# Splitting the first down-projection rows ahead of the last convolutions, in four pairs of slots

## The chip, the cores and the metric

The kernel runs on one core of a Trainium2 chip. It has a matrix engine (TensorE, PE in the profile), a vector engine (VectorE, DVE), a scalar engine (ScalarE, ACT), a general one (GpSimd, POOL) and a queue engine that issues the transfers (SyncE, SP). Each works through its own instructions in order. The metric is the device time of one execution in microseconds, the median of several runs.

## The reference, cut to what matters

One layer of a trunk: two recurrent mixers, and behind them a feed-forward block with a convolution. Only that block matters here:

```python
def _conv_ffn(h, w_up, conv_w, w_down, rows, cols):
    u = _dwconv2d(h @ w_up, conv_w, rows, cols)
    a, b = jnp.split(u, 2, axis=-1)
    return (jax.nn.silu(a) * b) @ w_down
...
    xl = xl + g2 * _conv_ffn(_modulate(_rmsnorm(xl, norm2_w[l]), sh2, sc2), w_up[l], ffn_conv_w[l],
                             w_down[l], rows, GRID_W)
    return _rmsnorm(xl, final_norm_w)
```

There are 1024 tokens of width 1024, the inner width is 2816 (22 blocks of 128), and the convolution is 3 x 3 over a 16 x 64 grid, one filter per channel.

## The kernel before

All matrix products are made in three matmuls of rounded parts: a factor x is held as xh (a cast to the fp32r format, on ACT) and xl = x - xh (a subtraction, called a split here, on DVE or POOL), and the product is xh wh + xh wl + xl wh. The weights get wh on ACT and wl on POOL in the same way.

The block's first loop runs over j = 0 to 21. For each j, `up(j)` and `up(22 + j)` multiply the input (kept in the 16 tiles L0 to L15: part k of it has its high half in L(2k) and its low half in L(2k+1)) into PSUM tiles of 128 channels x 1024 tokens, 48 matmuls each. `conv2` then makes the convolution: one scaled copy on ACT (L1483) and eight multiply-adds on DVE (L1490), each reading the tile before it. The first of the two goes into G[j] and through a Silu (L1548), the second into a tile cb, and POOL multiplies them (L1552). In the last j the PSUM tiles are copied to SBUF first (src, L1531), so that the down-projection can have their banks.

The second loop, the down-projection, runs over two halves `dh` of the output columns, and in each over c = 0 to 21, the rows of w_down in blocks of 128. `down_ops(c, dh, kind)` loads the weights (one transfer for two c), casts and splits them, casts G[c] (L1522) and splits it (L1523); 24 matmuls follow (L1575). For kind 1 the two halves of G[c] lie in slots of the tag L, which the input of the up-projection held before: L0, L1 for even c and L2, L3 for odd ones. For c = 0 of the first half (kind 0) there is a pair of tiles of its own. Slots of a weight cast are four, of a weight transfer three.

Who works when: PE's order in the down-projection is the text's. All other engines, and PE in the up-projection, get their order from a planner that walks through the program with estimated durations before the kernel is built; its order on each engine is then fixed. On the chip an engine whose next instruction isn't ready waits, with all that stands behind it.

At the end of the first half, DVE takes the result out of PSUM (L1595) and adds it to the residual (L1600), ACT squares it (L1602) and POOL multiplies it by a weight (L1611).

Of the kernel before, what the change touches and what calls it, by code (L numbers as in the profile page):

```python
# [10 lines left out]
F32R = mybir.dt.float32r  # L11
I32 = mybir.dt.int32
AF = mybir.ActivationFunctionType
ALU = mybir.AluOpType
# [3 lines left out]
P = 128  # L18
D = 1024
KD = D // P  # L20
T = 1024
# [9 lines left out]
NF = DFF // P  # L31
# [37 lines left out]
WARM = 4  # L69
NL = 4  # L70
NGL = 9
MOVE = ((0, 1, 2, 3), (4, 5, 6, 7))


@with_exitstack
def kernel(ctx: ExitStack, tc: tile.TileContext, A: dict, out: bass.AP):
# [3 lines left out]
    V, S, G, PE, SY = nc.vector, nc.scalar, nc.gpsimd, nc.tensor, nc.sync  # L80

    def pool(name, bufs=1, space=None, side=None):
        kw = {}
        if space is not None:
            kw["space"] = space
        if side is not None:
            kw["side"] = side
        return tc.tile_pool(name=name, bufs=bufs, **kw)
# [7 lines left out]
    def raw(ap):  # L96
        return ap.bitcast(F32)
# [24 lines left out]
    gd = dp.tile([P, P], F32, name="gd")  # L122
# [27 lines left out]
    def pl_tile(name):  # L150
        return ps2.tile([P, T], F32, name=name, tag="pl")
# [245 lines left out]
    pls = [pl_tile("pv0"), pl_tile("pv1")]  # L397
# [27 lines left out]
    pls = [pl_tile("pv0"), pl_tile("pv1")]  # L425
# [93 lines left out]
    def bcast_cols(dst, cols_, tiles):  # L519
        for g in range(2):  # L520
            p_ = tiles[g]
            for j in range(4):
                k = 4 * g + j
                PE.matmul(p_[:, j * P:(j + 1) * P], cols_[:, k:k + 1].to_broadcast([P, P]), ident, start=True, stop=True)
            S.copy(dst[:, g * 512:(g + 1) * 512], p_)
# [109 lines left out]
    with ExitStack() as es:  # L635
# [204 lines left out]
        def ml_prep(h, qt):  # L840
            Wt = []
            Qs = []
            for d in range(2):
                g4 = ml4.tile([P, NLT, P], F32, name="g4", tag="w4")
                SY.dma_start(out=g4, in_=gdv[h, d * 16 + NCX:d * 16 + NCH, :].partition_broadcast(P))
                w4 = ml4.tile([P, NLT, P], F32, name="w4t", tag="w4")
                V.tensor_tensor(w4, g4, mmask[:, d, :].unsqueeze(1).to_broadcast([P, NLT, P]), op=ALU.max)
                for c in range(NLT):
                    S.activation(w4[:, c, :], w4[:, c, :], AF.Exp, scale=-1.0, bias=U[:, d, NCX + c, h:h + 1])
                G.tensor_tensor(g4, g4, M[:, d, NCX:NCH, h:h + 1].to_broadcast([P, NLT, P]), op=ALU.subtract)  # L850
                S.activation(g4, g4, AF.Exp, scale=-1.0)
                V.tensor_tensor(g4, g4, qt.rearrange("p (c t) -> p c t", c=NLT), op=ALU.mult)
                Wt.append(w4)
                Qs.append(g4)
            return Wt, Qs
# [110 lines left out]
        pre = ml_prep(0, cur["q"])  # L966
        run(rnd1)
        flips = None
        for h in range(H):
# [10 lines left out]
            last = h == H - 1  # L980
            hs_ = ml_scan(h, cur, fill, RL if last else (R0 if h == 0 else R1), pre)
            pre = None
# [360 lines left out]
    with ExitStack() as es:  # L1343
# [94 lines left out]
        for ct in (0, NF):  # L1438
            halves = wq.pop(0)
            pl = pl_tile("pu")  # L1440
# [12 lines left out]
    def big_tile(i, name):  # L1453
        return pl_tile(name) if i % 4 < 2 else psb.tile([P, T], F32, name=name, tag="plb")


    lo = ctx.enter_context(pool("lo", side="left"))
    low = [[lo.tile([P, T], F32R, name=f"low{i}", tag=f"L{i}") for i in range(q, 2 * KD, 2)] for q in range(2)]
    Gp = ctx.enter_context(pool("G", side="left"))
    Gt = [Gp.tile([P, T], F32, name=f"G{j}") for j in range(NGL)]  # L1460
    g2bc = Gp.tile([P, D], F32, name="g2bc")
    with ExitStack() as es:
        fp = es.enter_context(pool("ff", bufs=2, side="left"))
        f1 = es.enter_context(pool("ff1", bufs=1, side="left"))
        bt = big_tile(2, "bt")
        bcast_cols(g2bc, mod2[:, 3 * KD:4 * KD], (bt[:, 0:512], bt[:, 512:1024]))
        fcw = f1.tile([P, 2 * NF, 9], F32, name="fcw")
        SY.dma_start(out=fcw, in_=A["ffcw"].rearrange("p (a b) -> p a b", b=9))

        def up(ct):  # L1470
            j, b = ct % NF, ct // NF
            if j == 0:
                return early[b][0]
            halves = split_weights(A["wup"][ct])
            pl = big_tile(2 * j + b, "pu")
            for g in range(2):
                up_half(pl, halves, g)
            return pl

        def conv2(acc, src, wcol):  # L1480
            a3 = acc.rearrange("p (r c) -> p r c", c=GW)
            s3 = src.rearrange("p (r c) -> p r c", c=GW)
            S.activation(acc, src, AF.Copy, scale=wcol(4))  # L1483
            for dy in (0, -1, 1):
                for dx in (-1, 0, 1):
                    if dy == 0 and dx == 0:
                        continue
                    r0, r1 = max(0, -dy), GH - max(0, dy)
                    c0, c1 = max(0, -dx), GW - max(0, dx)
                    V.scalar_tensor_tensor(  # L1490
                        a3[:, r0:r1, c0:c1], s3[:, r0 + dy:r1 + dy, c0 + dx:c1 + dx],
                        wcol((dy + 1) * 3 + dx + 1), a3[:, r0:r1, c0:c1], op0=ALU.mult, op1=ALU.add)

        pst = {}

        def g_pool(j):
            return Gp if j < NGL else Gr

        def down_ops(c, dh, kind):
            if c % 2 == 0:  # L1500
                st = wp.tile([P, 2, 512], F32, name="wst", bufs=3)
                SY.dma_start(out=st, in_=A["wdown"][dh, c // 2].rearrange("p (a b) -> p a b", a=2))
                pst["s"] = st
                if kind == 2:
                    pst["w"] = [g_pool(c - NF + NL + i).tile([P, 2, 512], F32R, name="wd", tag=f"G{c - NF + NL + i}")
                                for i in range(2)]
            src = pst["s"][:, c % 2, :]
            if kind == 2:
                wh, wl = [w[:, c % 2, :] for w in pst["w"]]
                gh, gl = [g_pool(j).tile([P, T], F32R, name="gd", tag=f"G{j}")  # L1510
                          for j in range(NL + 2 * (c - NF + NL), NL + 2 * (c - NF + NL) + 2)]
            else:
                wh = wp.tile([P, 512], F32R, name="wh", bufs=4)
                wl = wp.tile([P, 512], F32R, name="wl", bufs=4)
                if kind:
                    gh, gl = [lo.tile([P, T], F32R, name="gd", tag=f"L{2 * (c % 2) + i}") for i in range(2)]
                else:
                    gh = Gr.tile([P, T], F32R, name="gh")
                    gl = Gr.tile([P, T], F32R, name="gl")
            S.copy(wh, src)  # L1520
            G.tensor_tensor(wl, src, raw(wh), op=ALU.subtract)  # L1521
            S.copy(gh, Gt[c])  # L1522
            (G if dh == 0 and c < 3 else V).tensor_tensor(gl, Gt[c], raw(gh), op=ALU.subtract)  # L1523
            return gh, gl, wh, wl

        def up_src(ct, last):
            pl = up(ct)
            if not last:
                return pl
            src = fp.tile([P, T], F32, name="src", tag="cb")  # L1530
            S.copy(src, pl)  # L1531
            return src

        for j in range(NF):
            if j < len(MOVE):
                for k in MOVE[j]:
                    SY.dma_start(out=raw(low[0][k]), in_=raw(h2h[k]))
                    SY.dma_start(out=raw(low[1][k]), in_=raw(h2l[k]))
            if j == len(MOVE) + 1:
                h2h[:], h2l[:] = low  # L1540
                h2_cm.__exit__(None, None, None)
                Gr = ctx.enter_context(pool("Gr", side="right"))
                Gt.extend(Gr.tile([P, T], F32, name=f"G{i}") for i in range(NGL, NF))
            if j == NF - 1:
                pre0 = down_ops(0, 0, 0)
            pl = up_src(j, j == NF - 1)
            conv2(Gt[j], pl, lambda i: fcw[:, j, i:i + 1])
            S.activation(Gt[j], Gt[j], AF.Silu)  # L1548
            pl = up_src(NF + j, j == NF - 1)
            cb = fp.tile([P, T], F32, name="cb", tag="cb")  # L1550
            conv2(cb, pl, lambda i: fcw[:, NF + j, i:i + 1])
            G.tensor_tensor(Gt[j], Gt[j], cb, op=ALU.mult)  # L1552


# [5 lines left out]
    ms_cm.__enter__()  # L1560
    ys = [lo.tile([P, D], F32, name=f"y{t}", tag=f"L{4 + t}") for t in range(NLT)]
    s0 = d1.tile([P, NLT, 2], F32, name="s0")
    pre = [pre0]
    for dh in range(2):
        ds_ = slice(dh * 512, (dh + 1) * 512)
        pp = [big_tile(i, "pd") for i in range(NLT // 2)]
# [2 lines left out]
        def part(c, last, dh=dh):  # L1569
            return down_ops(c, dh, 2 if last else 1)  # L1570
# [34 lines left out]
        if dh == 0:  # L1605
            order = (0, 4, 1, 5, 2, 6, 3, 7)
            tmps = [evac(t) for t in order]
            pre = [part(c, False, 1) for c in range(2)]
# [109 lines left out]
```

## Time and profile before

| | us |
|---|---|
| median of 3 runs | 1572.02 (1570.85 to 1574.15) |
| profiled execution, own time | 1571.65 |
| its span | 1569.8 |
| PE busy | 1498.0 (95%) |
| DVE busy | 1112.2 (71%) |
| ACT busy | 543.4 (35%) |
| POOL busy | 599.6 (38%) |
| up-projection matmuls end | 1305.66 |

The up-projection with its convolutions takes the third quarter of the span, the down-projection the last 264 us. Times in the views are microseconds from the start of the span. Idle time of an engine costs only where the engine that bounds the stretch stands still with it.

### The profile page before, as it was taken

What the parts mean: (1) busy time and instruction counts of PE and PEld (TensorE: products, weight loads), DVE (VectorE), ACT (ScalarE), POOL (GpSimd) and SP (SyncE); (2) the same over time, 40 slices, a digit from 0 to 9 for tenths busy, and PEclk for the clock granted to TensorE, in tenths of its full rate; (3) what the DMA queues carried; (4) which work ended last, traced back from release to release, by engine and by line L of the source; (5) the groups of instructions that cost most, each with busy time, mean ns of one, the idle gap of its engine ahead of it and who ended that gap; (6) DMA issues with size and microseconds to landing.
All of it is one profiled execution on the core that took longest, in us unless ns stands there. A gap on an engine that the chain in (4) does not pass through costs nothing.

```text
span 1569.8 us, 22515 instructions
## 1 busy us (share of the span) xinstructions
PE 1498.0 (95%) x8934; PEld 1216.9 (78%) x8934; DVE 1112.2 (71%) x1460; ACT 543.4 (35%) x949; POOL 599.6 (38%) x510
## 2 busy tenths in 40 slices
PE   7899999998999999999999999999999998998997
PEld 4667788887877777777867888888888886886886
DVE  5777667779486776766587988989889898226334
ACT  4443243444143243434454222222222223233332
POOL 0073244554244644433322433332333325335341
PEclk8999999999999999999999999999999999999999
DMA  9246430222031111125567111111111104111102
GB/s 377 84 145 199 145 98 28 80 68 55 33 119 55 56 42 44 39 82 173 176 213 287 41 54 41 54 50 45 54 41 54 52 30 160 58 50 41 51 30 108
DMA packets 47935, 141.78 MB, mean 90 GB/s; under 512 B 4947, under 2 KB 15059, under 8 KB 47830
## 3 DMA queue, kind: packets, MB, share of 16 engines
q1 hardware_dynamic: 47830, 140.35, 26.5%
q8 instruction: 70, 1.15, 0.3%
q14 instruction: 35, 0.29, 0.1%
HBM read 119.81 MB, written 12.13 MB: 84 GB/s over the span
## 4 chain that ended last, share of the span: by engine, by line
PE 70%; DVE 7%; POOL 3%; ACT 3%; issue 2%; DMA 1%; POOLq 0%; SPq 0%; ACTq 0%; DVEq 0%
PE pu L1429 30%; PE pd L1575 13%; PE po L1285 3%; PE pl_hg L509 3%; PE pl_zb L509 3%; PE pl_zf L509 3%; PE pl_mo L509 2%; PE pl_mq L509 2%; PE pc L509 1%; PE pl_hq L509 1%; PE ap L1088 1%; DVE G L1490 1%; POOL QQ L1125 1%; PE st L876 1%; PE pl_mk L509 1%
## 5 line engine op out<-in xcount | busy, mean ns | idle before, releaser
L1429 PE MATMUL pu<-low,wh 128*128 128x512 f32 x1216 | 374.2, 389 | 0.0
L133 ACT CAST wh<-wst 128x512 fp32r<-128x512 f32 x184 | 112.0, 620 | 527.9 <-issue 227.2
L135 POOL TENSOR_TENSOR wl<-wst,wh 128x512 fp32r<-128x512 f32 x114 | 150.8, 1325 | 356.0 <-ACT wh L133 343.0
L1429 PEld LDWEIGHTS pu<-low,wh 128*128 128x128 f32 x1216 | 228.2, 188 | 47.4
L1429 PE MATMUL pu<-low,wl 128*128 128x512 f32 x608 | 236.5, 389 | 0.0
L1490 DVE SCALAR_TENSOR_TENSOR G<-pu,fcw,G 128x945 f32<-128x945 f32 (+2 forms) x168 | 205.3, 1222 | 23.9 <-ACT G L1483 19.1
L1490 DVE SCALAR_TENSOR_TENSOR cb<-pu,fcw,cb 128x945 f32<-128x945 f32 (+2 forms) x168 | 205.3, 1222 | 23.6 <-ACT cb L1483 18.8
L1575 PE MATMUL pd<-wh,gd 128*128 128x512 f32 x624 | 195.8, 395 | 11.6 <-DVE gd L1523 6.7
L1523 DVE TENSOR_TENSOR gd<-G,gd 128x1024 fp32r<-128x1024 f32 x41 | 56.8, 1386 | 129.7 <-ACT gd L1522 129.5
L1575 PEld LDWEIGHTS pd<-wh,gd 128*128 128x128 f32 x624 | 118.8, 191 | 37.9 <-DVE gd L1523 7.8
L1125 POOL TENSOR_TENSOR QQ<-QQ,FF 128x256 f32<-128x256 f32 x112 | 108.8, 993 | 80.7 <-PE ap L1088 38.0
L1429 PEld LDWEIGHTS pu<-low,wl 128*128 128x128 f32 x608 | 114.1, 188 | 23.7
L1575 PE MATMUL pd<-wl,gd 128*128 128x512 f32 x312 | 122.8, 394 | 0.0
L1521 POOL TENSOR_TENSOR wl<-wst,wh 128x512 fp32r<-128x512 f32 x40 | 73.2, 1833 | 113.8 <-ACT wh L1520 113.8
L135 DVE TENSOR_TENSOR wl<-wst,wh 128x512 fp32r<-128x512 f32 x70 | 57.7, 844 | 58.1 <-ACT wh L133 57.9
L1522 ACT CAST gd<-G 128x1024 fp32r<-128x1024 f32 x43 | 45.0, 1049 | 131.4 <-PE pd L1575 124.8
L1575 PEld LDWEIGHTS pd<-wl,gd 128*128 128x128 f32 x312 | 59.6, 191 | 12.5
L1118 DVE TENSOR_TENSOR KK<-KK,FF 128x768 f32<-128x768 f32 (+1 forms) x56 | 52.2, 942 | 15.2 <-PE tps L1104 11.8
L1552 POOL TENSOR_TENSOR G<-G,cb 128x1024 f32<-128x1024 f32 x22 | 53.9, 2452 | 14.9 <-DVE cb L1490 14.9
L874 POOL TENSOR_SCALAR kw<-ktok,WS 128x128 f32<-128x128 f32 x60 | 25.2, 422 | 49.2 <-PE st L876 48.9
L330 POOL TENSOR_TENSOR wl<-wst,wh 128x512 fp32r<-128x512 f32 x18 | 31.6, 1775 | 30.8 <-ACT wh L328 22.0
L1081 ACT COPY X<-KK 128x512 f32<-128x512 f32 x40 | 26.9, 682 | 47.0 <-DVE KK L1118 34.0
(390 smaller groups left out, 3078.3 us busy)
## 6 DMA issues: line engine op xcount, KB each, us to landing
wst<-in_wup_dram SPq DMA_DIRECT2D x44, 512.0 KB, 3.3
wst<-in_wcm_dram SPq DMA_DIRECT2D x28, 512.0 KB, 3.4
wst<-in_wmod_dram SPq DMA_DIRECT2D x26, 512.0 KB, 3.4
wst<-in_wout_dram SPq DMA_DIRECT2D x24, 512.0 KB, 3.6
wst<-in_wdown_dram SPq DMA_DIRECT2D x22, 512.0 KB, 3.4
wst<-in_wvml_dram SPq DMA_DIRECT2D x10, 512.0 KB, 6.0
x<-in_xcT_dram SPq DMA_DIRECT2D x8, 512.0 KB, 6.3
wsh<-in_wsh_dram SPq DMA_DIRECT2D x8, 512.0 KB, 10.1
```

The lines of the kernel that those rows point to most:

```text
L133: S.copy(wh, st[:, hs_])
L135: (eng or G).tensor_tensor(wl, st[:, hs_], raw(wh), op=ALU.subtract)
L509: PE.matmul(o, w[:, ws], x[k][:, c0:c1], start=(k == 0 and pi == 0), stop=(k == KD - 1 and pi == 2))
L1118: V.tensor_tensor(kv, kv, tk, op=ALU.mult)
L1125: G.tensor_tensor(qv, qv, tq, op=ALU.mult)
L1285: PE.matmul(po[g], x[k][:, ts_], halves[g][wi], start=(k == 0 and pi == 0), stop=(k == KD - 1 and pi == 2))
L1429: PE.matmul(pl[:, gs], w[:, ws], x[k][:, gs], start=(k == 0 and pi == 0), stop=(k == KD - 1 and pi == 2))
L1490: V.scalar_tensor_tensor(a3[:, r0:r1, c0:c1], s3[:, r0 + dy:r1 + dy, c0 + dx:c1 + dx], wcol((dy + 1) * 3 + dx + 1), a3[:, r0:r1, c0:c1], o ...
L1521: G.tensor_tensor(wl, src, raw(wh), op=ALU.subtract)
L1523: (G if dh == 0 and c < 3 else V).tensor_tensor(gl, Gt[c], raw(gh), op=ALU.subtract)
L1552: G.tensor_tensor(Gt[j], Gt[j], cb, op=ALU.mult)
L1575: PE.matmul(po[t], x[:, ts_], w, start=(c == 0 and pi == 0), stop=(c == NF - 1 and pi == 2))
```

## The change

`down_ops` for c = 1, 2 and 3 of the first half is called ahead of the last two convolutions instead of behind them. For that, both up-projections of the last j and their copies to SBUF come first. The tiles of G[c] go round four pairs of slots in the first half (L0, L2, L12, L14, each with its neighbour) and two pairs in the second. The splits of c = 0, 1, 2 of the first half, which POOL made, are made by DVE like all others.

```diff
+RING = ((0, 2, 12, 14), (0, 2))
...
                 if kind:
-                    gh, gl = [lo.tile([P, T], F32R, name="gd", tag=f"L{2 * (c % 2) + i}") for i in range(2)]
+                    gh, gl = [lo.tile([P, T], F32R, name="gd", tag=f"L{RING[dh][c % len(RING[dh])] + i}") for i in range(2)]
...
-            (G if dh == 0 and c < 3 else V).tensor_tensor(gl, Gt[c], raw(gh), op=ALU.subtract)
+            V.tensor_tensor(gl, Gt[c], raw(gh), op=ALU.subtract)
             return gh, gl, wh, wl
 
-        def up_src(ct, last):
+        def up_src(ct):
             pl = up(ct)
-            if not last:
-                return pl
             src = fp.tile([P, T], F32, name="src", tag="cb")
             S.copy(src, pl)
             return src
...
-            if j == NF - 1:
-                pre0 = down_ops(0, 0, 0)
-            pl = up_src(j, j == NF - 1)
-            conv2(Gt[j], pl, lambda i: fcw[:, j, i:i + 1])
+            if j < NF - 1:
+                pls = [up(j), None]
+            else:
+                pre = [down_ops(0, 0, 0)]
+                pls = [up_src(j), up_src(NF + j)]
+                pre += [down_ops(c, 0, 1) for c in range(1, 4)]
+            conv2(Gt[j], pls[0], lambda i: fcw[:, j, i:i + 1])
             S.activation(Gt[j], Gt[j], AF.Silu)
-            pl = up_src(NF + j, j == NF - 1)
             cb = fp.tile([P, T], F32, name="cb", tag="cb")
-            conv2(cb, pl, lambda i: fcw[:, NF + j, i:i + 1])
+            conv2(cb, pls[1] or up(NF + j), lambda i: fcw[:, NF + j, i:i + 1])
             G.tensor_tensor(Gt[j], Gt[j], cb, op=ALU.mult)
...
-    pre = [pre0]
```

## Rows read from the trace of the kernel before

**Rows 1.** The page: busy us (share); a group: xcount, busy us, mean ns.
```profile
PE 1498.0 (95%) x8934; PEld 1216.9 (78%) x8934; DVE 1112.2 (71%) x1460; ACT 543.4 (35%) x949; POOL 599.6 (38%) x510
...
L135 POOL TENSOR_TENSOR wl<-wst,wh 128x512 fp32r<-128x512 f32 x114 | 150.8, 1325 | 356.0 <-ACT wh L133 343.0
```

**Rows 2.** Waits of PE, 1255 to 1570 us: us in total, times, longest.
```profile
PE pd L1575 <- DVE gd L1523: 6.7, 2, 6.2
```

**Rows 3.** Timeline of PE: start, us, instruction, [idle before <- releaser].
```profile
1305.66 0.39 PE L1575 MATMUL pd<-wh,gh 128*128 128x512 f32 x1
...
1311.25 0.39 PE L1575 MATMUL pd<-wh,gd 128*128 128x512 f32 x1
...
1328.97 1.22 PE L1575 MATMUL pd<-wh,gd 128*128 128x512 f32 x2 [6.22 <-DVE gd L1523]
...
1449.54 0.80 PE L1575 MATMUL pd<-wh,gd 128*128 128x512 f32 x1 [4.89 <-ACT gd L1522]
```

**Rows 4.** Windows around the wait: busy of each engine, PE clock, DMA.
```profile
1294.81:1305.69 10.88, 10.88 (x50) 9.00 (x49) 8.89 (x5) 5.21 (x7) 7.13 (x4) 1.00 0.51 168
...
1317.00:1340.00 23.00, 16.78 (x68) 13.42 (x66) 15.02 (x11) 5.19 (x8) 10.51 (x5) 0.85 0.37 137
```

**Rows 5.** Timeline of ACT, 1301 to 1336 us.
```profile
1301.09 2.00 ACT L1522 CAST gd<-G 128x1024 fp32r<-128x1024 f32 x2 [3.57 <-PE pu L1429]
...
1306.21 1.01 ACT L1531 COPY src<-pu 128x1024 f32<-128x1024 f32 x1
1314.97 1.06 ACT L1548 ACTIVATE G<-G 128x1024 f32<-128x1024 f32 x1 [7.75 <-DVE G L1490]
...
1317.48 1.05 ACT L1522 CAST gd<-G 128x1024 fp32r<-128x1024 f32 x1
...
1335.66 1.05 ACT L1522 CAST gd<-G 128x1024 fp32r<-128x1024 f32 x1 [11.99 <-PE pd L1575]
```

**Rows 6.** Timeline of DVE, 1285 to 1331 us.
```profile
1285.65 10.03 DVE L1490 SCALAR_TENSOR_TENSOR cb<-pu,fcw,cb 128x1008 f32<-128x1008 f32 x8 [0.92 <-ACT cb L1483]
1297.56 17.32 DVE L1490 SCALAR_TENSOR_TENSOR G<-src,fcw,G 128x1008 f32<-128x1008 f32 x8 [1.88 <-ACT G L1483]
1317.16 10.62 DVE L1490 SCALAR_TENSOR_TENSOR cb<-src,fcw,cb 128x1008 f32<-128x1008 f32 x7 [2.28 <-ACT cb L1483]
1327.69 1.22 DVE L1523 TENSOR_TENSOR gd<-G,gd 128x1024 fp32r<-128x1024 f32 x1
1328.83 1.20 DVE L1490 SCALAR_TENSOR_TENSOR cb<-src,fcw,cb 128x945 f32<-128x945 f32 x1
1329.94 1.22 DVE L1523 TENSOR_TENSOR gd<-G,gd 128x1024 fp32r<-128x1024 f32 x1
```

**Rows 7.** The chain of waits in order of time: start, us, what.
```profile
1297.56 2.69 DVE G L1490
...
1302.81 3.26 DVE G L1490
...
1306.09 3.24 DVE G L1490
...
1309.36 2.13 DVE G L1490
```

**Rows 8.** Timeline of POOL at 894 us and 1302 to 1331 us.
```profile
894.88 2.41 POOL L1523 TENSOR_TENSOR gl<-G,gh 128x1024 fp32r<-128x1024 f32 x1 [0.66 <-ACT gh L1522]
...
1302.22 6.10 POOL L1523 TENSOR_TENSOR gd<-G,gd 128x1024 fp32r<-128x1024 f32 x2 [3.06 <-ACT gd L1522]
1308.29 4.33 POOL L1521 TENSOR_TENSOR wl<-wst,wh 128x512 fp32r<-128x512 f32 x2
1330.10 3.31 POOL L1552 TENSOR_TENSOR G<-G,cb 128x1024 f32<-128x1024 f32 x1 [8.31 <-DVE cb L1490]
```

**Rows 9.** Timeline of DVE, two convolutions ready at once.
```profile
855.03 1.21 DVE L1490 SCALAR_TENSOR_TENSOR G<-pu,fcw,G 128x960 f32<-128x960 f32 x1
856.15 1.19 DVE L1490 SCALAR_TENSOR_TENSOR cb<-pu,fcw,cb 128x945 f32<-128x945 f32 x1
```

## Prediction

> **What bounds the kernel now.** I read the page first. TensorE (PE) is busy 95% of the span [rows 1], so a change to the splits can pay only where PE stands. The waits of PE from 1255 us to 1570 us, the whole end of the kernel behind the last up-projections, are headed by the waits for a split on VectorE (DVE, L1523), longest 6.2 us [rows 2]. PE's timeline puts that one inside the first half: the matmul at 1328.97 us waits 6.22 us; one more wait of size, 4.89 us for a cast on ScalarE (ACT, L1522), stands at 1449.54 us, where the second half begins [rows 3]. From here c counts the rows of the down-projection, as in the code.
>
> What does the wait cost in all? The last tile of the up-projection, 48 matmuls (2 halves of 8 k of 3), is one window of 10.88 us at full clock, so one matmul takes 0.2267 us and one c of 24 matmuls 5.44 us; from 1317 us to 1340 us the granted clock averages 0.85 [rows 4]. At the lower of its two levels (1.2 GHz; 2.4 GHz is full) for some of it, that makes 0.15 x 23 / 0.5 = 6.9 us, part of them inside the wait, when there was no work to slow. So I take the loss from the end of a later row. c=0 starts at 1305.66 and c=1 at 1311.25 [rows 3]; without a wait c=3 ends at 1311.25 + 3 x 5.44 = 1327.57. In the trace the cast that reuses c=3's slots starts at 1335.66 [rows 5], some 0.04 us behind the matmul that frees them. So the stall takes 1335.62 - 1327.57 = 8.05 us: 6.22 us idle, and the other 1.8 us the slow matmuls right behind it.
>
> Why is that split late? DVE is in order, and it starts the split at 1327.69, behind seven of the eight multiply-adds of the last convolution, though its cast started at 1317.48 [rows 5, 6]. The convolutions themselves are late: in the steady state eight multiply-adds take 10.03 us, but the G convolution of the last column takes 17.32 us [rows 6]. The chain of waits shows its pieces: 2.69 us for the first, 3.26 and 3.24 us beside the two splits that GpSimd (POOL) runs there, 2.13 us beside a weight split, where an undisturbed one elsewhere takes 1.21 us [rows 7 to 9]. Only here does the source lie in SBUF (src, not pu).
>
> **The change, part by part.** *The splits of c=0, 1, 2 go from POOL to DVE.* POOL's two at 1302.22 take 6.10 us [rows 8] and lengthen two multiply-adds by 3.26 + 3.24 - 2 x 1.21 = 4.08 us [rows 7]. On DVE each costs 1.22 us [rows 6], with 0.02 us between two instructions: 2 x 1.24 = 2.48 us. DVE gains 1.6 us. The split of c=0 ran at 894.88 on POOL [rows 8]; 1.24 us more on DVE is there against the 0.92 us that DVE idles at each convolution [rows 6], so it is made good within two convolutions, and the four PSUM buffers keep PE from noticing: 0.
>
> By the Trainium skill (SBUF — State Buffer, Who interferes with whom), a DVE instruction with two SBUF inputs and a GpSimd instruction that reads SBUF hold the shared port by turns, and one blocks fully until the other is done. The rows here agree in kind (2.13 us against 1.21 us), but by that rule each POOL operation costs DVE its whole own length, 1.3 us for a weight split [rows 1], and not 0.92 us; it would move a rival below, not the sum.
>
> *Four pairs of slots in place of two.* c=1, 2, 3 now take L2, L12, L14, and c=4 takes L0. These hold the k=1, 6, 7 and 0 parts of the input of the up-projection, whose last matmuls end at 1305.66 [rows 3]. Today the casts of two rows go at 1301.09, as soon as PE is through with k=0 and 1, and the third must wait for c=1's matmuls: 1317.48 [rows 5]. With four pairs nothing waits for a down-projection matmul before c=5. The second half of that tile begins at 1300.2; its 3 matmuls per k take 0.68 us and free k=0 at about 1300.9, k=1 at 1301.6, k=6 at 1305.0 and k=7 at 1305.7, so the casts of c=4, 1, 2, 3, at 1.05 us each with the src copy between them, end by about 1309. PE needs c=3 at 1311.25 + 2 x 5.44 = 1322.1 and c=4 at 1327.6.
>
> *The splits of c=1 to 3 stand in the program ahead of both convolutions.* What matters is where they come in DVE's queue. The order that the planner writes is not the text's: where two convolutions are ready it alternates between them, multiply-add by multiply-add [rows 9], so whatever is ready is put in behind the instruction that runs. I expect all four splits (c=1 to 4) among the G convolution's multiply-adds. DVE then runs: from 1297.56 the first, 2.69; seven more at 1.24, 8.7; four splits, 5.0; two weight splits of POOL at 2.13 - 1.21 = 0.92 each, 1.8. It ends at 1315.8, 0.9 us later than today. After today's pause of 2.28 us [rows 6], eight multiply-adds take 9.9 us, the splits of c=5 and 6 2.5 us, and three weight splits up to 2.8 us: the last convolution ends at about 1333. PE doesn't see it, because c=4 is split by 1316 (needed 1327.6), and c=5 by about 1322 (needed 1333.0).
>
> *The src copy of the last up-projection comes ahead of the casts.* It must free PSUM before the fourth bank pair of c=0 is written, 18 matmuls behind 1305.66, at 1309.9. It ends at 1307.2 today [rows 5] and by 1308 after: 0. Its DMA, and those of the weights, keep their order in SP's queue: 0.
>
> *An unknown: reading from L12 to L15.* c=0 lies in another pool and its 24 matmuls take 5.59 us in place of 5.44 us [rows 3]. If two rows of four ran so, ten rows would lose 10 x 0.15 = 1.5 us. L12 to L15 lie in the same pool as L0 to L3, whose c takes 5.44 us, so I take 0 and keep 1.5 us for the range.
>
> *What is late next.* After it PE runs through until the wait of 4.89 us [rows 3], which the change leaves: the second half keeps two pairs. It moves earlier with PE.
>
> **The sum.** Minus 6.2 us of wait, minus 1.8 us of slow matmuls: the profiled execution goes from 1571.65 to 1563.6 us. The median of the runs lies 0.4 us over the profiled one, so 1572.02 - 8.05 = 1564.0 us. The range of one's own for this case is 1562 to 1566: the runs before spread by some 1.5 us to either side, and 1.5 us are open for L12 to L15.
>
> **Rivals.** *The split of c=4 comes behind both convolutions* (chance 0.15). Today DVE's next split comes right behind the last multiply-add [rows 6]. Then DVE is done with the convolutions near 1330, the split at 1331, and PE waits 1331 - 1327.6 = 3.4 us, plus up to 1.8 us of clock: 1567.4 to 1569.2.
>
> *A weight split waits on POOL behind the last product* (0.06). POOL is in order too. If the split of c=6's weights stands behind the product (3.31 us; two weight splits took 4.33 us [rows 8]), it ends at 1333 + 3.3 + 2.2 = 1338.5, against a need at 1338.7: no cost by the rows, by a margin of 0.2 us. With a DVE 2 us later than I make it, it costs 1.8 us: 1565.8.
> By the rule of the Trainium skill above (SBUF — State Buffer, Who interferes with whom), with 0.4 us more for each of five POOL operations, it would be those 2 us later, 1565.8 too.
>
> *DVE follows the text, slower than before* (0.06). If the three splits stand in DVE's queue ahead of every multiply-add, DVE waits for the cast of c=3 until 1309, where today it works from 1297.56. The G convolution then ends at 1310 + 9.9 + 1.8 = 1322, the other one at 1322 + 2.3 + 9.9 + 1.8 = 1336, and the split of c=4 behind it at 1337.3: PE waits 9.7 us plus 1.8 us, 1564.0 + 11.5 = 1575.5. It decides from the point where that split ends later than 1327.6 + 6.2 = 1333.8. Against it: rows 9.
>
> *The wait stays as it is* (0.07): if the casts of c=3 or 4 sit in ACT's queue behind the Silu, which itself waits for DVE (1314.97 today [rows 5]), DVE splits late as before: 1572.0.
>
> *The second half's start is planned anew too* (0.04), since four pairs let the first half's last rows be done early, and the 4.9 us with 1.8 us of clock behind them go as well: 1564.0 - 6.7 = 1557.3.
>
> My forecast has 0.62. A change of 0.2%, 3.1 us, is about what a measurement of this kernel can tell from none, so faster means under 1568.9. To it go the forecast, the POOL rival, the re-planned half and four fifths of the first rival: 0.62 + 0.06 + 0.04 + 0.12 = 0.84. Same: 0.03 + 0.07 and a sixth of the text-order case, 0.11. Slower: 0.05. The range from 1561.5 to 1569 holds the forecast, the POOL rival and nearly all of the first rival, 0.82.
>
> **What would show it.** Right: no PE wait above 1 us between 1305 us and the end of the first half; the granted clock 1.00 there; c=3's matmuls ending near 1327.6; the first half ending 8 us earlier; four DVE splits before the last multiply-add of the G convolution, and that convolution without pieces above 3 us. Wrong: a PE wait for L1523 near 1327 or 1333, a DVE idle stretch between 1298 and 1309, a c of 5.59 us in rows with L12 to L15, or a longer wait than 4.9 us where the second half starts.

## The result, and the profile after

The changed kernel takes 1564.04 us (median of 7 runs, 1558.78 to 1567.81) against 1574.15 us for the kernel before on the same chip (7 runs, 1570.85 to 1578.58): a ratio of 0.9928, 95% interval 0.9905 to 0.995. A second comparison of the same two (11 runs and 15) gives 0.9947, 0.9931 to 0.9964; a sixteenth run of the kernel before, 1680.26 us at a mean clock of 0.846, is left out of it. The ratios rest on all the other runs of both kernels and can differ a little from the quotient of the two medians. Forecast were 1564.0 us and, as a ratio, 1564.0 / 1572.02 = 0.9949.

The waits of PE from 1255 us to the end, us in total, times, longest:

```profile
PE pd L1575 <- ACT gd L1523: 4.9, 1, 4.9
PE pd L1575 <- DVE gd L1524: 0.5, 1, 0.5
```

The wait of 6.2 us for a DVE split [rows 2] is gone; the one at the start of the second half stands. (The lines of the kernel have moved by one: the cast is now L1523, the split L1524.) PE's timeline, the first matmul of the down-projection and the one that ends that wait:

```profile
1303.47 0.39 PE L1575 MATMUL pd<-wh,gh 128*128 128x512 f32 x1
...
1439.23 0.80 PE L1575 MATMUL pd<-wh,gd 128*128 128x512 f32 x1 [4.89 <-ACT gd L1523]
```

Call the time between these two F. It is 135.76 us here and was 1449.54 - 1305.66 = 143.88 us [rows 3]: 8.12 us less, where the prediction worked out 8.05. The windows, in the columns of [rows 4], show PE busy throughout and at its full 2.4 GHz:

```profile
1303.40:1423.20 119.80, 119.80 (x529) 99.05 (x529) 48.80 (x40) 35.13 (x45) 42.65 (x23) 1.00 0.24 81
...
1317.00:1340.00 23.00, 23.00 (x103) 19.06 (x102) 18.52 (x13) 7.03 (x10) 12.63 (x6) 1.00 0.21 69
```

The spans of the two profiles differ by more, 1569.8 - 1559.4 = 10.4 us. Of the rest, 2.19 us are already there when the down-projection begins (1305.66 against 1303.47), behind a stretch in which PE's instructions and their order are the same in both kernels. Over the 14 profiled executions of this study, which all have that same stretch on PE, the first matmul of the down-projection starts between 1301.83 and 1311.54 us: 1303.47 and 1309.48 in two executions of the changed kernel alone. So these 2 us are scatter from run to run, and F, which leaves it out, is the better measure; it repeats (135.76 and 135.75 us in two executions of the changed kernel).

DVE's timeline, for [rows 6]:

```profile
1295.36 6.47 DVE L1491 SCALAR_TENSOR_TENSOR G<-src,fcw,G 128x1008 f32<-128x1008 f32 x4 [1.88 <-ACT G L1484]
1301.76 3.45 DVE L1524 TENSOR_TENSOR gd<-G,gd 128x1024 fp32r<-128x1024 f32 x2
1305.13 3.35 DVE L1491 SCALAR_TENSOR_TENSOR G<-src,fcw,G 128x945 f32<-128x945 f32 x2
1308.40 1.21 DVE L1524 TENSOR_TENSOR gd<-G,gd 128x1024 fp32r<-128x1024 f32 x1
1309.54 1.20 DVE L1491 SCALAR_TENSOR_TENSOR G<-src,fcw,G 128x960 f32<-128x960 f32 x1
1310.66 2.31 DVE L1524 TENSOR_TENSOR gd<-G,gd 128x1024 fp32r<-128x1024 f32 x1
1312.89 1.19 DVE L1491 SCALAR_TENSOR_TENSOR G<-src,fcw,G 128x945 f32<-128x945 f32 x1
1316.37 4.72 DVE L1491 SCALAR_TENSOR_TENSOR cb<-src,fcw,cb 128x1008 f32<-128x1008 f32 x3 [2.29 <-ACT cb L1484]
1321.01 1.21 DVE L1524 TENSOR_TENSOR gd<-G,gd 128x1024 fp32r<-128x1024 f32 x1
1322.14 5.97 DVE L1491 SCALAR_TENSOR_TENSOR cb<-src,fcw,cb 128x960 f32<-128x960 f32 x4
1328.04 1.22 DVE L1524 TENSOR_TENSOR gd<-G,gd 128x1024 fp32r<-128x1024 f32 x1
```

Four splits stand between the multiply-adds of the G convolution, and two in the second convolution. The view doesn't name their rows; by the order in which the slots come free (L0, L2, L12, L14) they are c = 4, 1, 2, 3, and then c = 5 and 6. ACT's casts, for [rows 5], show why they can:

```profile
1298.90 2.01 ACT L1523 CAST gd<-G 128x1024 fp32r<-128x1024 f32 x2 [3.57 <-PE pu L1430]
...
1302.98 1.05 ACT L1523 CAST gd<-G 128x1024 fp32r<-128x1024 f32 x1 [1.56 <-PE pu L1430]
...
1305.36 1.05 ACT L1523 CAST gd<-G 128x1024 fp32r<-128x1024 f32 x1
...
1314.18 1.06 ACT L1550 ACTIVATE G<-G 128x1024 f32<-128x1024 f32 x1 [4.29 <-DVE G L1491]
```

All four are done by 1306.4, before the Silu that waits for DVE; the cast of c=3 was behind it before. POOL, for [rows 8], has two weight splits behind its last product:

```profile
1330.44 3.32 POOL L1553 TENSOR_TENSOR G<-G,cb 128x1024 f32<-128x1024 f32 x1 [7.07 <-DVE cb L1491]
1333.72 3.53 POOL L1522 TENSOR_TENSOR wl<-wst,wh 128x512 fp32r<-128x512 f32 x2
```

### The profile page after: what moved, and what is told of

It is laid out like the page before. It is cut to its first block, busy times and chain, and to the rows that moved or that the text cites. A ratio compares the mean times of both kernels' runs of the same rounds, so it can differ in the third digit from the quotient of the medians.

```text
span 1559.4 us, 22506 instructions
## 1 busy us (share of the span) xinstructions
PE 1493.8 (96%) x8934; PEld 1213.8 (78%) x8934; DVE 1111.4 (71%) x1463; ACT 543.8 (35%) x949; POOL 586.8 (38%) x507
## 4 chain that ended last, share of the span: by engine, by line
PE 72%; DVE 6%; ACT 2%; issue 2%; POOL 2%; DMA 2%; POOLq 0%; ACTq 0%; DVEq 0%; SPq 0%
PE pu L1430 31%; PE pd L1575 14%; PE po L1286 3%; PE pl_hg L510 3%; PE pl_zb L510 3%; PE pl_zf L510 3%; PE pl_mo L510 2%; PE pl_mq L510 2%; PE pc L510 1%; PE pl_hq L510 1%; PE ap L1089 1%; POOL QQ L1126 1%; PE st L877 1%; PE pl_mk L510 1%; PE nd L921 1%
## 5 line engine op out<-in xcount | busy, mean ns | idle before, releaser
L1524 DVE TENSOR_TENSOR gd<-G,gd 128x1024 fp32r<-128x1024 f32 x43 | 63.0, 1469 | 120.9 <-ACT gd L1523 120.8
L1523 ACT CAST gd<-G 128x1024 fp32r<-128x1024 f32 x43 | 45.0, 1049 | 116.9 <-PE pd L1575 108.6
## 6 DMA issues: line engine op xcount, KB each, us to landing
wsh<-in_wsh_dram SPq DMA_DIRECT2D x8, 512.0 KB, 10.1
```

Of the source, the lines that this page charges most:

```text
L1524: V.tensor_tensor(gl, Gt[c], raw(gh), op=ALU.subtract)
```

## The experiments

The change has three parts: four pairs of slots (SLOTS), splits of c = 0 to 2 on DVE (DVE), and the calls ahead of the convolutions (TEXT). Each was made alone, and each was undone alone. All kernels compute the full result.

**SLOTS alone**

```diff
+RING = ((0, 2, 12, 14), (0, 2))
-gh, gl = [lo.tile(..., tag=f"L{2 * (c % 2) + i}") for i in range(2)]
+gh, gl = [lo.tile(..., tag=f"L{RING[dh][c % len(RING[dh])] + i}") for i in range(2)]
```

> Only the four pairs of slots are added to the kernel before; the splits of c=0 to 2 stay on POOL and the text keeps its order. F is the time from the first matmul of the down-projection to the matmul that ends the wait at the start of the second half: 143.9 us in the kernel before, 135.8 us in the changed one. My theory now: the planner puts a split into DVE's queue where its cast becomes ready, so the slots alone decide; the splits of c=3 and 4 come ahead of the last convolution, no PE wait in the first half, F 135.8 us and the full gain of 8 us. Rival A (the order of the text decides): the wait of 6.2 us stays, F 143.9 us. Rival B (POOL's port contention decides): DVE is as late as before, 3 us or more of the wait stay, F above 139 us.

Measured: 1564.48 us, ratio 0.9933 (0.9914 to 0.9952), F = 1439.24 - 1303.48 = 135.76 us: all of the gain. PE's waits show only the second half's. DVE's timeline:

```profile
1301.75 3.42 DVE L1524 TENSOR_TENSOR gd<-G,gd 128x1024 fp32r<-128x1024 f32 x1
1305.09 8.90 DVE L1491 SCALAR_TENSOR_TENSOR G<-src,fcw,G 128x945 f32<-128x945 f32 x4
1313.91 1.22 DVE L1524 TENSOR_TENSOR gd<-G,gd 128x1024 fp32r<-128x1024 f32 x1
1316.28 9.37 DVE L1491 SCALAR_TENSOR_TENSOR cb<-src,fcw,cb 128x1008 f32<-128x1008 f32 x6 [1.15 <-ACT cb L1484]
```

The split of c=4 comes in the G convolution and that of c=3 ahead of the last one (1313.91; before, it stood behind seven of that convolution's multiply-adds). POOL still holds DVE up: four multiply-adds take 8.90 us here. Rivals A and B fall.

**DVE alone**

```diff
-(G if dh == 0 and c < 3 else V).tensor_tensor(gl, Gt[c], raw(gh), op=ALU.subtract)
+V.tensor_tensor(gl, Gt[c], raw(gh), op=ALU.subtract)
```

> Only the engine of the splits of c=0 to 2 is changed, from POOL to DVE; two pairs of slots and the old text. Theory of the slots: the cast of c=3 still waits for c=1's matmuls, so its split stays inside the last convolution; DVE is only somewhat earlier, by the 1.6 us of the splits and by standing two multiply-adds further forward in the queue, so the wait falls from 6.2 to about 2.4 us, F 138 to 140 us. Rival A (text order): 6.2 us stay, F 143.9. Rival B (POOL contention): the wait goes, F 135.8.

Measured: 1568.55 us, ratio 0.9969 (0.9952 to 0.9986), F = 1443.90 - 1305.80 = 138.10 us. PE's timeline:

```profile
1324.93 0.73 PE L1575 MATMUL pd<-wh,gd 128*128 128x512 f32 x2 [2.05 <-DVE gd L1523]
```

A wait of 2.05 us where 2.4 were expected. The split of c=3 stands behind five multiply-adds of the last convolution in place of seven, and that convolution starts earlier (DVE's timeline). ACT's cast of c=3 now stands idle for a matmul of c=1, which holds its slots:

```profile
1315.61 8.13 DVE L1490 SCALAR_TENSOR_TENSOR cb<-src,fcw,cb 128x1008 f32<-128x1008 f32 x5 [2.28 <-ACT cb L1483]
1323.65 1.22 DVE L1523 TENSOR_TENSOR gd<-G,gd 128x1024 fp32r<-128x1024 f32 x1
...
1316.80 1.06 ACT L1522 CAST gd<-G 128x1024 fp32r<-128x1024 f32 x1 [0.77 <-PE pd L1575]
```

**TEXT alone** (the changed kernel with `RING = ((0, 2), (0, 2))` and the old engine rule)

> Only the text is reordered (both up-projections of the last j and the calls for c=1 to 3 ahead of the convolutions); two pairs of slots, splits of c=0 to 2 on POOL. Theory of the slots: nothing changes, wait 6.2 us, F 143.9 us, total as before. Rival A (text order): the wait goes, F 135.8 us. Rival B: nothing changes.

Measured: 1572.93 us, ratio 0.9994 (0.9979 to 1.0009), F = 1448.27 - 1304.59 = 143.68 us. The wait is unchanged, and DVE's split of c=3 stands where it stood:

```profile
1316.08 10.62 DVE L1491 SCALAR_TENSOR_TENSOR cb<-src,fcw,cb 128x1008 f32<-128x1008 f32 x7 [2.28 <-ACT cb L1484]
1326.62 1.22 DVE L1524 TENSOR_TENSOR gd<-G,gd 128x1024 fp32r<-128x1024 f32 x1
```

**All but SLOTS** (`RING = ((0, 2), (0, 2))` in the changed kernel)

> The changed kernel with two pairs of slots in place of four. Theory of the slots: as with the engine alone, a wait of about 2.4 us for the split of c=3, F 138 to 140 us. Rival A (text order) and rival B (POOL contention) both: no wait, F 135.8 us.

Measured: 1568.35 us, ratio 0.9966 (0.9949 to 0.9984), F = 1451.37 - 1311.54 = 139.83 us. PE's timeline:

```profile
1330.77 0.74 PE L1575 MATMUL pd<-wh,gd 128*128 128x512 f32 x2 [2.14 <-DVE gd L1524]
```

The wait is that of DVE alone within 0.1 us, as the theory of the slots has it.

**All but DVE** (the old engine rule in the changed kernel)

> The changed kernel with the splits of c=0 to 2 on POOL again. Theory of the slots: no PE wait in the first half, F 135.8 us, the full gain of 8 us; but the G convolution shows multiply-adds of over 3 us again and ends about 2 us later than in the changed kernel, off PE's path. Rival B (POOL contention decides): a wait of 3 us or more returns, F above 139 us.

Measured: 1564.15 us, ratio 0.994 (0.9916 to 0.9963), F = 1442.49 - 1306.73 = 135.76 us. POOL lengthens the multiply-adds again (one takes 3.2 us), and PE doesn't notice. That the G convolution would end 2 us later was wrong: it ends 10.5 us behind the first matmul of the down-projection, in the changed kernel 10.6, since the changed kernel has three more DVE splits among those multiply-adds (four against one).

**All but TEXT** (the kernel before with SLOTS and DVE)

> The changed kernel with the text in its old order. Theory of the slots: no PE wait in the first half, F 135.8 us, the same gain as the changed kernel. Rival A (text order decides): the wait of 6.2 us returns, F 143.9 us.

Measured: 1563.58 us, ratio 0.9936 (0.9916 to 0.9956), F = 1441.29 - 1305.52 = 135.77 us.

The table of F, in us, with the wait for a split in the first half:

| | F | wait |
|---|---|---|
| kernel before | 143.88 | 6.22 |
| TEXT | 143.68 | 6.22 |
| DVE | 138.10 | 2.05 |
| TEXT and DVE | 139.83 | 2.14 |
| SLOTS | 135.76 | none |
| SLOTS and TEXT | 135.76 | none |
| SLOTS and DVE | 135.77 | none |
| all three (the change) | 135.76 | none |

**The clock behind a short wait.** By F, TEXT and DVE together lose 1.7 us more than DVE alone, with all but the same wait (the ratios of the totals, 0.9966 and 0.9969, can't tell them apart). Each was profiled once more:

> The changed kernel with two pairs of slots, a second look at the clock. In the first look a wait of 2.14 us was followed by slow matmuls that cost 1.9 us more; with the engine change alone a wait of 2.05 us was followed by hardly any (0.3 us). If the fall of the clock follows from the length of the wait, the same 1.9 us return. If it is chance, either may come.

> The kernel before with DVE for the splits of c=0 to 2, a second look at the clock behind its wait of some 2 us: 0.3 us of slow matmuls as in the first look if the length of the wait decides, either 0.3 or 1.9 us if it is chance.

Windows of 10.23 us from the matmul behind the wait, TEXT and DVE, in the first execution and the second (waits of 2.14 and 2.13 us):

```profile
1330.77:1341.00 10.23, 10.23 (x38) 8.27 (x39) 6.10 (x5) 1.57 (x2) 6.43 (x3) 0.83 0.16 51
```

```profile
1325.13:1335.36 10.23, 10.23 (x38) 8.32 (x39) 6.10 (x5) 1.57 (x2) 6.43 (x3) 0.83 0.16 51
```

And DVE alone (2.05 and 2.07 us):

```profile
1324.93:1335.16 10.23, 10.23 (x45) 8.49 (x46) 6.47 (x5) 1.57 (x2) 6.60 (x3) 1.00 0.16 51
```

```profile
1327.18:1337.41 10.23, 10.23 (x45) 8.48 (x46) 6.47 (x5) 1.57 (x2) 6.60 (x3) 1.00 0.15 51
```

Both executions of a kernel agree: 38 matmuls in the window and a mean clock of 0.83, or 45 and 1.00; F repeats too, 139.83 us both times against 138.10 and 138.14. The seven matmuls' worth are 1.6 us. The same outcome twice speaks against chance, but two kernels with 0.06 to 0.09 us between their waits can't say what makes the difference: that stays open.

**The wait that is left.** At the start of the second half of the changed kernel the cast of c=2 stands on ACT behind eight squares, and its split on DVE behind eight additions and that cast:

```profile
1438.15 1.03 ACT L1523 CAST gd<-G 128x1024 fp32r<-128x1024 f32 x1
...
1425.98 11.45 DVE L1600 TENSOR_TENSOR y<-y,ytmp 128x512 f32<-128x512 f32 x8
1439.21 3.87 DVE L1524 TENSOR_TENSOR gd<-G,gd 128x1024 fp32r<-128x1024 f32 x2 [1.78 <-ACT gd L1523]
```

Three kernels try what removed the first wait, on top of the changed kernel, which ran beside two of them once more:

> The changed kernel once more, beside the two that follow. F, from the first matmul of the down-projection to the matmul that ends the wait at the start of the second half, 135.8 us; total 0.5% under the kernel before, that is 8 us, if the 2.2 us by which its profile was ahead before the down-projection began are chance; 0.65% if they are lasting.

Measured: 1563.88 us, ratio 0.9947 (0.9931 to 0.9964), F = 1445.23 - 1309.48 = 135.75 us. The total lies 0.5% under the kernel before and not 0.65%, so the 2.2 us were chance. From the first matmul of the down-projection to the end of the span it takes 1566.1 - 1309.48 = 256.62 us, the first execution of the changed kernel 1559.4 - 1303.47 = 255.93 us: the three kernels that follow are measured so against the shorter of the two.

*Order: three rows called ahead in place of two*

```diff
-pre = [part(c, False, 1) for c in range(2)]
+pre = [part(c, False, 1) for c in range(3)]
```

> The changed kernel, with the call for row c=2 of the second half moved ahead of the additions of the first half's end (three rows called ahead in place of two). The wait of 4.9 us there: the cast of c=2 now stands behind three squares on ACT in place of eight, its split behind seven additions on DVE in place of eight. Expected: the wait falls from 4.9 us to about 3 us, because DVE's additions, 1.4 us each beside POOL's products, still stand ahead of the split; F about 133 to 134 us. If ACT's queue alone made the wait, it would go entirely and F be 129.

Measured: 1557.55 us, ratio 0.9923 (0.9901 to 0.9945), F = 1436.39 - 1301.83 = 134.56 us, half a microsecond over the range. F ends later in the row here: the first two matmuls of c=2 now run before the wait. From the first matmul to the end it takes 1554.7 - 1301.83 = 252.87 us, 3.1 us less than the changed kernel. The wait falls to 3.23 us and is now one for DVE; ACT's queue was only a part of it:

```profile
1436.39 1.04 PE L1575 MATMUL pd<-wh,gd 128*128 128x512 f32 x2 [3.23 <-DVE gd L1524]
```

*Slots: c=2 of the second half in the pair that c=0 of the first half left empty*

```diff
-if kind:
-    gh, gl = [lo.tile(..., tag=f"L{RING[dh][c % len(RING[dh])] + i}") for i in range(2)]
+if kind and not (dh == 1 and c == 2):
+    gh, gl = [lo.tile(..., tag=f"L{RING[dh][(c - (dh == 1 and c > 2)) % len(RING[dh])] + i}") for i in range(2)]
 else:
     gh = Gr.tile([P, T], F32R, name="gh")
```

> The changed kernel with row c=2 of the second half in the pair of tiles left empty by c=0 of the first, and still only two rows of the second half called ahead. If the wait at the start of the second half is one of slots, c=2 has none any more; the cast of c=3 comes behind the eight squares on ACT, its split behind the eight additions, at about the time PE needs it: a wait of 0.4 to 1 us, total 1 us or less above the version that also calls four rows ahead (1554.7). If the order of the calls decides, the wait stays at 3 to 5 us, total 1557 to 1564.

Measured: 1555.95 us, ratio 0.9896 (0.9878 to 0.9914). All waits of PE from 1285 us on:

```profile
PE pd L1575 <- DVE gd L1524: 0.6, 1, 0.6
```

From the first matmul to the end it takes 1554.3 - 1305.50 = 248.80 us, 7.1 us less than the changed kernel.

*Slots and order: the same, with four rows called ahead*

> The changed kernel with four rows of the second half called ahead, and row c=2 of the second half in the pair of tiles that c=0 of the first half had (it is empty by then), so that its cast and split need not wait for a matmul of the second half. Rows from c=3 on take the two pairs in turn. If the 4.9 us wait is one of slots, as the first was, it goes, with the slow matmuls behind it: F falls by 4.9 + 0.5 us of waits and some 1.8 us of clock, to 128.6 us, and the total by 7 us, to 1557. If it only moves on to c=3, F stays above 132.

Measured: 1554.73 us, ratio 0.9893 (0.9874 to 0.9911). There is no PE wait in the down-projection any more, and the clock stays at full:

```profile
1305.66:1541.00 235.34, 235.34 (x1038) 194.46 (x1037) 104.56 (x87) 78.83 (x116) 94.03 (x65) 1.00 0.19 65
```

From the first matmul to the end it takes 1553.5 - 1305.66 = 247.84 us, 8.1 us less than the changed kernel, with 7 forecast. This version beats both kernels: on the same chip, beside it, the changed one stood at 0.9947. From the slots alone (0.9896) it can't be told apart by the ratio; by one profile of each, the order adds 1.0 us.

## Why the prediction was right, point by point

**What the wait costs: right.** 8.05 us were worked out from where the row c=3 would end; F fell by 8.12 us. The idle time in the profile was 6.22 us; the other 1.9 us were slow matmuls, which the windows show gone (0.85 in [rows 4], 1.00 now). That the median came out at 1564.04, against 1564.0 forecast, is luck in part: single runs of the changed kernel spread from 1558.78 to 1567.81 us, wider than the range of 1562 to 1566, and the kernel before stood at 1574.15 beside it and not at 1572.02, which makes the fall of the medians 10.1 us. F is the firmer test.

**Where the splits go: right.** Four of them are among the G convolution's multiply-adds. The last of those multiply-adds ends at 1314.1, and 2.19 us must be added to compare with the times of before: 1316.3 against 1315.8 forecast. The split of c=5 ends at 1322.2, or 1324.4 in the times of before, and not at 1322: it stands behind three multiply-adds. PE needed it at 1333.0.

**What each part does: the slots alone carry it.** The prediction had all three parts work together and did not split the gain between them. Two of its explanations have to be cut down. That the splits "stand in the program ahead of both convolutions" does nothing by itself: TEXT alone leaves the order of DVE's queue around the wait as it was, ratio 0.9994. That DVE is late because POOL holds it up is half a cause: DVE alone brings 143.88 - 138.10 = 5.8 us of the 8.1, but on top of the slots nothing, because with four pairs the splits come so early that lateness doesn't count. The two are no sum: either cuts the same wait, and the slots cut it whole.

One reading of the prediction needs care: that the cast of c=3 went at 1317.48 because it had to wait for c=1's matmuls. Those end at 1311.25 + 5.44 = 1316.69; the cast then stood in ACT's queue behind the Silu [rows 5] and two more instructions. It was done at 1318.53, 9.2 us before its split began. So on the chip PE waited for the split's place in DVE's queue, and the slots matter because that place changes with their number (SLOTS alone). That the planner sets the place by when it expects the slot to come free fits the queues shown above, but its estimated times are in no trace, so this step is argued and not shown. A split of c=3 put right behind its cast with only two pairs of slots was not tried; by an estimate from these rows (1318.53 + 1.22) it would have been done near 1320, ahead of 1322.75, where PE's wait began.

The Trainium skill (Perfetto Trace Analysis, Optimization Strategy) says that consistent bubbles, the same gap repeating on the engine that should be saturated, "can mean there isn't enough SBUF/PSUM for the next tile to be allocated". Here it was one gap and not a repeated one, and the releaser that the profile names is a DVE split; that slots were short shows only further back, in the casts. In the kernel before, the one behind that of c=3 stands idle for a matmul:

```profile
1322.11 1.05 ACT L1522 CAST gd<-G 128x1024 fp32r<-128x1024 f32 x1 [3.06 <-PE pd L1575]
```

**The engine move's price: right where it could be seen.** DVE was to gain 1.6 us. With two pairs, the G convolution ends 9.22 us behind the first matmul of the down-projection before, and 1313.32 - 1305.80 = 7.52 us with DVE alone: 1.7 us.

By the Trainium skill (SBUF — State Buffer, Who interferes with whom) the port that DVE and GpSimd share is an exclusive lock. The trace agrees: POOL's weight split, begun at 1309.96 beside a multiply-add (1309.54, 1.20 us), takes 1.93 us against 1.29 us undisturbed; DVE's split, begun at 1310.66 beside that weight split, takes 2.31 us against 1.21 us undisturbed and ends 1.08 us behind it. So a POOL operation costs DVE about what is left of it when DVE's instruction begins, 1.10 us here and 0.92 us in the row of before, and not the whole 1.3 us that the prediction drew from the rule.

**The rivals.** The split of c=4 was not behind the convolutions; DVE did not follow the text; ACT's casts were not behind the Silu. On POOL two weight splits are behind the last product, but the first of them is c=7's, with 5.44 us more to spare. The second half's start was not planned anew, and its 4.89 us stayed.

**L12 to L15: no loss.** The first half's 22 rows would take 5.59 + 21 x 5.44 = 119.83 us if all rows but c=0 ran at the rate of L0 to L3; from the first matmul of c=0 (1303.47) to the first of the second half (1423.30) it is 119.83 us.

## What to carry to other kernels

When an engine waits for an instruction that is late in another's queue, follow it one step further: what does its input need, and when could it be ready at the earliest? Here the number of slots decided. Two more pairs removed the first wait by themselves (8.1 us), where a new order of the text alone brought nothing and another engine alone 5.8 us. At the next wait one spare pair alone brought 7.1 us, calling one more row ahead alone 3.1 us, and the spare pair with two more rows called ahead 8.1 us. In a program whose order a planner writes, moving lines may change nothing, so look in the trace whether the queue has changed. Cost a wait from where the work behind it ends, since its slow matmuls (1.9 us here behind 6.2 us) are not in the idle time.

## What the runs showed of the hardware

- Waits of nearly the same length (2.05 and 2.07 us with DVE alone; 2.13 and 2.14 us with TEXT and DVE) were followed by full clock in the one kernel and by a mean of 0.83 over 10.23 us in the other, in both profiled executions of each. The wait of 0.64 us in the version with the spare pair was followed by full clock (1.00 over the next 10.23 us).
- DVE and POOL went by turns: with SLOTS alone a POOL split, begun at 1301.00 beside a DVE multiply-add (1300.61, 1.22 us), took 3.09 us against 2.41 us undisturbed [rows 8]. The DVE split begun at 1301.75 beside it took 3.42 us against 1.21 us and ended 1.08 us behind it, about its own length.
- The time at which the down-projection begins varies by 9.7 us over 14 executions with the same instructions on PE ahead of it (1301.83 to 1311.54), and F behind it, in the four kernels without a wait in the first half and with the old start of the second, by 0.02 us.
